# First phase of a decoder block on one core: x in four tiles of 4 KB rows, modulation rows between them, and half of x's transposes behind the first product

## The chip, the cores and the metric

The kernel runs on one core of a Trainium2 chip. The metric is the device time of one execution in microseconds (us). The engines are TensorE (PE in the profile, PEld for its weight loads), VectorE (DVE), ScalarE (ACT), GpSimd (POOL) and SyncE (SP), which issues most of the DMAs.

## What is computed

One layer of a residual decoder block for 512 tokens of width 1024 in float32. The change touches only the first lines: the norm, the modulation of x by the vector c, and the order in which the first projections start.

```
c_act = jax.nn.silu(c)
mod = c_act @ ada_w[l] + ada_b[l]
shift1, scale1, gate1, shift2, scale2, gate2 = ...
h = rms_norm(x, norm1_g[l]) * (1 + scale1) + shift1
z = h @ w_in[l]
q, k, v, p, g_attn, g_pool = jnp.split(z, split_at, axis=-1)
...
x = x + gate1 * (merged @ w_out[l])
...
x = x + gate2 * ((jax.nn.silu(u_g) * u_v) @ w_down[l])
```

## The kernel before, in words

All of it is one function, `block_kernel`. The instructions of PE, DVE and ACT stand on each engine in the order in which the code is written; an instruction that waits holds up all that stand behind it on its engine. SP's DMAs too are issued in the order of the code.

The first phase makes h, transposed: eight channel tiles k = 0 to 7 of 128 channels by 512 tokens. It runs so:

- x is loaded as four token tiles t = 0 to 3 of 128 rows, each in two halves of 512 channels (eight DMAs of 256 KB, line 154). `rms_rows` sums the squares of one half on ACT (L164) and of the other on DVE (L166), adds them (`ms`, L170) and raises to the power -1/2 on POOL (`rs`, L172). `scale_x` multiplies the halves by it (L210 and L214 on ACT, L212 on DVE).
- PE transposes 32 blocks of 128 by 128 (L232) into eight PSUM banks, xT_0 to xT_7. There are eight banks in all.
- The modulation is not a product on PE. silu(c), `crow`, is spread over the partitions by two small matmuls (`cb`, L220) and copied to `cbc`. Each of 16 rows of weights, `raw_ada`, of 513 KB, is multiplied by `cbc` and summed on DVE (`ada_sum`, L181). Its result is a column `acol`: g = 0 is the shift, g = 1 the scale, of channel tile k. Row (0, k) is loaded as `raw_ada_k` and row (1, k) as `raw_ada_(8+k)`.
- `make_x(k)` copies xT_k out of PSUM with the norm's gain (`xs_k`, L238 on ACT, and L240 on DVE for k = 7). `make_h(k)` applies scale and shift (L270) and rounds to the high part `h_k_h` (L272), both on ACT; `lo_h(k)` subtracts on DVE for the low part `h_k_l` (L277). For k = 0 gain and scale are one factor, `gs`.
- The projections p and q need weights in the same two parts: `hi_of` rounds a raw tile (`hi_p0`, L97 or L99), and a subtraction gives `lo_p0` (L109). A product is three matmuls: high by high (L125 for p and q), high by low, low by high (L128).
- PE then runs, for k = 0 to 7, twelve matmuls of p (four banks p_0 to p_3) and twelve of q (banks q_0 to q_3), and goes on with the projection k (L118 to L120).

The raw tiles (`raw_ada`, `raw_p`, `raw_q`, `crow`) share five buffers. `pump` issues the next load of a written list, `queue`, as soon as one of them is given free by `ada_sum` or `split`. The subtraction of q1's weights is on POOL (`pool=("q1",)`); four memsets of `kz` come later on the same engine.

Of the kernel before, what the change touches and what calls it, by code (L numbers as in the profile page):

```python
# [48 lines left out]
def block_kernel(tc, x, cvec, ada, wtok, wch, pool_w, wbr, wout, wup, wdn, pack, table, out):  # L49
# [4 lines left out]
    with ctx:  # L54
# [91 lines left out]
        acol = cpool.tile([P, 48], F32, name="acol")  # L146


        xt = []
        for t in range(TT):  # L150
            row = []
            for f in range(2):
                xi = slot(f"x_{t}_{f}")
                nc.sync.dma_start(xi, x[t * P : (t + 1) * P, f * 512 : (f + 1) * 512])
                row.append(xi)
            xt.append(row)

        def rms_rows(tiles, name):

            ss = mini.tile([P, 2], F32, tag="ss", name=f"ss_{name}")  # L160
            for f in range(2):
                junk = slot(f"junk_{name}_{f}")
                if f == 0:
                    nc.scalar.activation(junk, tiles[f], AF.Square, scale=1.0 / math.sqrt(D), accum_out=ss[:, f : f + 1])  # L164
                else:
                    nc.vector.tensor_tensor_reduce(  # L166
                        out=junk, in0=tiles[f], in1=tiles[f], op0=ALU.mult, op1=ALU.add, scale=1.0 / D,
                        scalar=EPS, accum_out=ss[:, f : f + 1])
            ms = mini.tile([P, 1], F32, tag="ms", name=f"ms_{name}")
# [37 lines left out]
        rss, cbs = [], []

        def scale_x(t):
            nc.scalar.activation(xt[t][0], xt[t][0], AF.Copy, scale=rss[t])  # L210
            if t < TT - 1:
                nc.vector.tensor_scalar(xt[t][1], xt[t][1], rss[t], None, op0=ALU.mult)  # L212
            else:
                nc.scalar.activation(xt[t][1], xt[t][1], AF.Copy, scale=rss[t])  # L214

        for t in range(TT):
            rs = rms_rows(xt[t], f"x{t}")
            if t < 2:
                cbs.append(bank(f"cb_{t}"))
                nc.tensor.matmul(cbs[t], ones, crow[:, t * 512 : t * 512 + 512], start=True, stop=True)  # L220
            if t:
                scale_x(t - 1)
                if t < 3:
                    nc.scalar.activation(cbc[:, (t - 1) * 512 : t * 512], cbs[t - 1], AF.Copy)
            rss.append(rs)
        scale_x(TT - 1)

        hh, hl, xs, araw = [], [], {}, {}
        xT = [bank(f"xT_{k}") for k in range(KT)]
        for t in range(TT):  # L230
            for k in range(KT):
                nc.tensor.transpose(  # L232
                    xT[k][:, tslice(t)], xt[t][k // 4][:, (k % 4) * P : (k % 4 + 1) * P], ident)

        def make_x(k):
            xs[k] = slot(f"xs_{k}")
            if k < KT - 1:
                nc.scalar.activation(xs[k], xT[k], AF.Copy, scale=col(C_N1 + k))  # L238
            else:
                nc.vector.tensor_scalar(xs[k], xT[k], col(C_N1 + k), None, op0=ALU.mult)  # L240


        queue = [(0, 0), (1, 0), "p0", "q0", (0, 1), (1, 1), (0, 2), (1, 2), "p1", "q1", (0, 3), (1, 3),
                 (0, 4), (1, 4), (0, 5), (1, 5), "p2", "q2", (0, 6), (1, 6), (0, 7), (1, 7), "p3", "q3"]
        held = [0]

        def pump():
            while queue and held[0] < 5:
                it = queue.pop(0)
                if isinstance(it, str):  # L250
                    early[it] = load_unit(plan[pos[it]][0], it)
                else:
                    araw[it] = ada_load(it[0], it[1])
                held[0] += 1

        def sum_h(k):
            for g in range(2):
                ada_sum(g, k, araw[g, k])
                held[0] -= 1
                pump()  # L260

        def split(name, **kw):
            ahead(name, 0, pool=("q1",), **kw)
            held[0] -= 1
            pump()

        def make_h(k, src=None, scale=None):
            hi = slot(f"h_{k}_h", F32R)
            lo = slot(f"h_{k}_l", F32R)
            nc.scalar.activation(xs[k], xs[k] if src is None else src, AF.Identity,  # L270
                                 scale=acols(1, k) if scale is None else scale, bias=acols(0, k))
            nc.scalar.activation(hi, xs[k], AF.Copy)  # L272
            hh.append(hi)
            hl.append(lo)

        def lo_h(k):
# [608 lines left out]
```

## Time and profile before

| | us |
|---|---|
| median of 3 runs (lowest to highest) | 691.81 (691.68 to 691.94) |
| the profiled execution, its own time | 691.4 |
| its span, first to last instruction | 689.6 |
| PE busy in the span | 677.6 (98%) |
| DVE busy | 443.2 (64%) |
| ACT busy | 304.4 (44%) |
| POOL busy | 59.4 (9%) |
| bytes moved by DMA | 94.50 MB, 137 GB/s over the span |

PE is the engine that is nearly always busy. The other shares are means over stages that differ, so they don't tell who is waited for at the start.

### The profile page before, as it was taken

To read this page: it belongs to the slowest core of one execution; us is meant where nothing else is said; L and a number is where in the kernel's file an instruction comes from. 1 tells how busy PE (TensorE), PEld (TensorE's weight loads), DVE (VectorE), ACT (ScalarE), POOL (GpSimd) and SP (SyncE) were. 2 spreads that over 40 slices of the span, in tenths; PEclk is the share of its full clock that TensorE was granted. 3 is DMA by queue.
4 is the path that set the end of the run, shared out by engine and by line. 5 is a ranking of instruction groups with operands and counts; after the bars stand their busy time and mean duration, and the time that the engine had idled before them with its cause. 6 is when DMAs were issued, how large, how long until landed. Compare 5 with 4: busy or idle time off the path is not lost.

```text
span 689.6 us, 8494 instructions
## 1 busy us (share of the span) xinstructions
PE 677.6 (98%) x3238; PEld 566.5 (82%) x3238; DVE 443.2 (64%) x719; ACT 304.4 (44%) x490; POOL 59.4 (9%) x60
## 2 busy tenths in 40 slices
PE   6999999999999999999999999999999999999997
PEld 4788788888888788889988888888888888888886
DVE  5786776887878788786575767676565653225213
ACT  6555347666555556315653434435343442211110
POOL 2203140000000155311000000000000000000000
PEclk9999999999999999999999999999999999999999
DMA  8795241454542466750313354442323324224001
GB/s 307 277 337 201 71 143 43 145 191 138 150 141 93 155 227 203 244 210 32 122 62 122 99 177 131 145 159 86 122 85 100 113 71 153 92 92 152 31 1 61
DMA packets 27631, 94.50 MB, mean 137 GB/s; under 512 B 3283, under 2 KB 3708, under 8 KB 27590
## 3 DMA queue, kind: packets, MB, share of 16 engines
q1 hardware_dynamic: 26198, 89.63, 38.1%
q0 software_dynamic: 1392, 4.33, 2.2%
q8 instruction: 25, 0.41, 0.2%
q14 instruction: 16, 0.13, 0.1%
HBM read 91.83 MB, written 2.12 MB: 136 GB/s over the span
## 4 chain that ended last, share of the span: by engine, by line
PE 94%; DMA 2%; ACT 1%; DVE 1%; SPq 1%; issue 1%; DVEq 0%; ACTq 0%
PE u L119 12%; PE u L120 12%; PE u L118 12%; PE d L118 6%; PE d L119 6%; PE d L120 6%; PE gate_ps L120 4%; PE gate_ps L119 4%; PE gate_ps L118 4%; PE o L118 2%; PE o L119 2%; PE o L120 2%; DMA raw_ada<-in_ada 2%; PE O L485 2%; PE p L128 1%; PE q L128 1%
## 5 line engine op out<-in xcount | busy, mean ns | idle before, releaser
L118 PE MATMUL u<-h2h,hi_up 128*128 128x512 f32 (+1 forms) x384 | 142.7, 372 | 0.0
L119 PE MATMUL u<-h2l,hi_up 128*128 128x512 f32 (+1 forms) x384 | 142.6, 371 | 0.0
L120 PE MATMUL u<-h2h,lo_up 128*128 128x512 f32 (+1 forms) x384 | 142.6, 371 | 0.0
L118 PEld LDWEIGHTS u<-h2h,hi_up 128*128 128x128 f32 x384 | 72.3, 188 | 12.6
L119 PEld LDWEIGHTS u<-h2l,hi_up 128*128 128x128 f32 x384 | 72.3, 188 | 12.5
L120 PEld LDWEIGHTS u<-h2h,lo_up 128*128 128x128 f32 x384 | 72.3, 188 | 12.3
L118 PE MATMUL d<-hi_dn,y_h 128*128 128x512 f32 (+1 forms) x198 | 72.6, 367 | 0.0
L119 PE MATMUL d<-lo_dn,y_h 128*128 128x512 f32 (+1 forms) x198 | 72.6, 367 | 0.0
L120 PE MATMUL d<-hi_dn,y_l 128*128 128x512 f32 (+1 forms) x198 | 72.4, 365 | 0.0
L109 DVE TENSOR_TENSOR lo_dn<-raw_dn,hi_dn 128x1024 fp32r<-128x1024 f32 x22 | 26.6, 1224 | 61.6 <-ACT hi_dn L99 61.6
L181 DVE CUSTOM_DVE_ANT_0 raw_ada<-raw_ada,cbc 128x1026 f32<-128x1026 f32 x48 | 61.1, 1292 | 3.3 <-DMA raw_ada<-in_ada 3.3
L109 DVE TENSOR_TENSOR lo_up<-raw_up,hi_up 128x1024 fp32r<-128x1024 f32 x44 | 52.1, 1221 | 8.7 <-ACT hi_up L99 8.7
L99 ACT ACTIVATE hi_dn<-raw_dn 128x1024 fp32r<-128x1024 f32 x22 | 23.0, 1059 | 75.0 <-PE d L120 66.2
L740 ACT ACTIVATE uv<-u,pk 128x512 f32<-128x512 f32 x22 | 17.2, 780 | 87.5 <-PE u L120 87.5
L741 DVE SCALAR_TENSOR_TENSOR uv<-u,pk,uv 128x511 f32<-128x511 f32 x22 | 16.5, 749 | 52.9 <-ACT uv L740 52.9
L120 PE MATMUL gate_ps<-h_h,lo_gate 128*128 128x512 f32 x128 | 49.9, 390 | 0.0
L119 PE MATMUL gate_ps<-h_l,hi_gate 128*128 128x512 f32 x128 | 49.9, 390 | 0.0
L118 PE MATMUL gate_ps<-h_h,hi_gate 128*128 128x512 f32 x128 | 49.9, 390 | 0.0
L99 ACT ACTIVATE hi_up<-raw_up 128x1024 fp32r<-128x1024 f32 x44 | 44.1, 1047 | 4.3 <-PE u L119 4.3
L118 PEld LDWEIGHTS d<-hi_dn,y_h 128*128 128x128 f32 x198 | 37.4, 189 | 6.2
L120 PEld LDWEIGHTS d<-hi_dn,y_l 128*128 128x128 f32 x198 | 37.3, 188 | 6.2
L119 PEld LDWEIGHTS d<-lo_dn,y_h 128*128 128x128 f32 x198 | 37.4, 189 | 6.1
(202 smaller groups left out, 1234.3 us busy)
## 6 DMA issues: line engine op xcount, KB each, us to landing
raw_ada<-in_ada SPq DMA_DIRECT2D x48, 513.0 KB, 4.8
raw_up<-in_wup SPq DMA_DIRECT2D x44, 512.0 KB, 4.3
raw_dn<-in_wdn SPq DMA_DIRECT2D x22, 512.0 KB, 3.3
raw_gate<-in_wch SPq DMA_DIRECT2D x16, 512.0 KB, 5.0
raw_br<-in_wbr SPq DMA_DIRECT2D x8, 512.0 KB, 4.4
raw_wo<-in_wout SPq DMA_DIRECT2D x8, 512.0 KB, 3.2
x<-in_x SPq DMA_DIRECT2D x8, 256.0 KB, 4.2
raw_p<-in_wtok SPq DMA_DIRECT2D x4, 512.0 KB, 5.9
```

The source lines that it names most:

```text
L99: nc.scalar.activation(hi, raw, AF.Copy)
L109: (nc.gpsimd if nm in pool else nc.vector).tensor_sub(lo, raw, hi.bitcast(F32))
L118: nc.tensor.matmul(ps, sh, mh, start=start, stop=False)
L119: nc.tensor.matmul(ps, sh, ml, start=False, stop=False)
L120: nc.tensor.matmul(ps, sl, mh, start=False, stop=stop)
L128: nc.tensor.matmul(ps, sl if i else sh, mh if i else ml, start=False, stop=stop and i != late)
L181: nc.vector.tensor_tensor_reduce(out=raw, in0=raw, in1=cbc, op0=ALU.mult, op1=ALU.add, scale=1.0, scalar=0.0, accum_out=acol[:, i : i + 1])
L485: nc.tensor.matmul(ops[:, kt * P :], lw, m[b_][:, o : o + w], start=(i == 0 and j == 0), stop=(i == 3 and j == 1))
L740: nc.scalar.activation(t, ps, AF.Identity, scale=cw(2), bias=col(C_CB + i))
L741: nc.vector.scalar_tensor_tensor(t[:, 1:], ps[:, : S - 1], cw(1), t[:, 1:], op0=ALU.mult, op1=ALU.add)
```

## The change

x comes as four DMAs of 512 KB with rows of 4 KB, into buffers of the pools for high and low weight parts, which are still free then. The order of loads becomes x_0, x_1, the modulation rows (0, 0) and (1, 0), x_2, x_3, p0, q0. The code of the phase is written anew in another order: the first modulation sums stand between the norm's sums of x; only the blocks of channel tiles 0 to 3 are transposed ahead of p's k = 0, and those of 4 to 7 stand behind it (`flip_x(t, 4)`), in the banks that held xT_0 to xT_3. `make_x(4)` to `make_x(7)` stand behind those. p's k = 0 takes its low weights ahead of the low part of h (`late`). The rounding of q0 goes from ACT to DVE, the subtraction of q1 from POOL to DVE. For k = 0 high part and value both come straight from PSUM, one on ACT (L300) and one on DVE (L304).

```diff
-            for f in range(2):
-                xi = slot(f"x_{t}_{f}")
-                nc.sync.dma_start(xi, x[t * P : (t + 1) * P, f * 512 : (f + 1) * 512])
...
+            xi = (whi_p if t < 2 else wlo_p).tile([P, 1024], F32, tag="hi" if t < 2 else "lo", name=f"x_{t}")
+            nc.sync.dma_start(xi, x[t * P : (t + 1) * P])
...
-        queue = [(0, 0), (1, 0), "p0", "q0", (0, 1), (1, 1), (0, 2), (1, 2), "p1", "q1", (0, 3), (1, 3),
+        queue = [(0, 0), (1, 0), "x2", "x3", "p0", "q0", (0, 1), (1, 1), (0, 2), (1, 2), "p1", "q1", (0, 3), (1, 3),
...
-            ahead(name, 0, pool=("q1",), **kw)
+            ahead(name, 0, **kw)
...
+        def flip_x(t, k0):
+            for k in range(k0, k0 + 4):
+                nc.tensor.transpose(xT[k][:, tslice(t)], xt[t][:, k * P : (k + 1) * P], ident)
...
+        flip_x(0, 0)
+        flip_x(1, 0)
+        sum_one(0, 0)
+        rss.append(rms_rows(xh[2], "x2"))
+        sum_one(1, 0)
...
+        rss.append(rms_rows(xh[3], "x3"))
+        scale_x(2, 0, False)
+        his["p0"] = hi_of("p0", early["p0"], True)
+        scale_x(3, 0, True)
+        flip_x(2, 0)
+        flip_x(3, 0)
...
+        nc.scalar.activation(hh[0], xT[0], AF.Identity, scale=gs, bias=acols(0, 0))
+        scale_x(2, 1, False)
+        scale_x(3, 1, False)
+        split("p0")
+        nc.vector.tensor_scalar(xs[0], xT[0], gs, acols(0, 0), op0=ALU.mult, op1=ALU.add)
         lo_h(0)
-        for k in range(1, KT):
-            if k == 5:
-                his["q0"] = hi_of("q0", early["q0"])
+        for k in range(1, 4):
             make_x(k)
         sum_h(1)
+        his["q0"] = hi_of("q0", early["q0"], True)
         split("q0")
         make_h(1)
         lo_h(1)
         sum_h(2)
-        qps = [bank(f"q_{t}") for t in range(TT)]
         pps = [bank(f"p_{g}") for g in range(TT)]
...
+            if k == 0:
+                for k2 in range(4, KT):
+                    xT[k2] = bank(f"xT_{k2}")
+                for t in range(TT):
+                    flip_x(t, 4)
+                for k2 in range(4, KT):
+                    make_x(k2, k2 == 7)
+                qps = [bank(f"q_{t}") for t in range(TT)]
```

What this makes of the order is shown at three places. In the rows the text after "<-" is what is read, the numbers behind the names are buffer numbers, and the brackets name the engines and DMA lanes that the instruction waits for. The first place is PE where p's k = 0 ends and q's begins. Before:

```order
L128 MATMUL p_2_272<-h_0_h_218,lo_p0_224 128x512
L128 MATMUL p_3_273<-h_0_h_218,lo_p0_224 128x512
L125 MATMUL q_0_266<-hi_q0_237,h_0_h_218 128x512 [waits Activation_49]
L125 MATMUL q_1_267<-hi_q0_237,h_0_h_218 128x512
L125 MATMUL q_2_268<-hi_q0_237,h_0_h_218 128x512 [waits Activation_49]
L125 MATMUL q_3_269<-hi_q0_237,h_0_h_218 128x512 [waits Activation_49]
L128 MATMUL q_0_266<-hi_q0_237,h_0_l_219 128x512
```

Now, with the last eight of the sixteen moved transposes:

```order
L259 MATMUL xT_4_246<-pk_80,x_2_101 128x128
L259 MATMUL xT_5_247<-pk_80,x_2_101 128x128
L259 MATMUL xT_6_248<-pk_80,x_2_101 128x128
L259 MATMUL xT_7_249<-pk_80,x_2_101 128x128
L259 MATMUL xT_4_246<-pk_80,x_3_103 128x128
L259 MATMUL xT_5_247<-pk_80,x_3_103 128x128
L259 MATMUL xT_6_248<-pk_80,x_3_103 128x128
L259 MATMUL xT_7_249<-pk_80,x_3_103 128x128
L125 MATMUL q_0_274<-hi_q0_213,h_0_h_190 128x512 [waits DVE_49,Activation_49]
L125 MATMUL q_1_275<-hi_q0_213,h_0_h_190 128x512 [waits Activation_49]
L125 MATMUL q_2_276<-hi_q0_213,h_0_h_190 128x512 [waits Activation_49]
L125 MATMUL q_3_277<-hi_q0_213,h_0_h_190 128x512 [waits DVE_49]
```

The transposes of channel tiles 4 to 7 now stand between p's k = 0 and q's k = 0, and q's banks are those of xT_4 to xT_7: the first matmul into q_3 waits for DVE, which copies xT_7 out.

The second place is DVE from the low part of h's tile 0 to the first sum of k = 2. Before:

```order
L277 TENSOR_TENSOR h_0_l_219<-xs_0_217,h_0_h_218 128x512 [waits Activation_49]
L240 TENSOR_SCALAR xs_7_243<-xT_7_166,pk_80 128x512 [waits PE_49]
L181 ISA raw_ada_1_207,acol_91<-raw_ada_1_207,cbc_81 128x1026 [waits DMAHW5_49]
L181 ISA acol_91 128x1
L181 ISA raw_ada_9_210,acol_91<-raw_ada_9_210,cbc_81 128x1026 [waits DMAHW7_49]
L181 ISA acol_91 128x1
L109 TENSOR_TENSOR lo_q0_251<-raw_q0_205,hi_q0_237 128x1024 [waits DMAHW4_49,Activation_49]
L277 TENSOR_TENSOR h_1_l_256<-xs_1_229,h_1_h_255 128x512 [waits Activation_49]
L181 ISA raw_ada_2_213,acol_91<-raw_ada_2_213,cbc_81 128x1026 [waits DMAHW0_49]
```

Now:

```order
L255 TENSOR_TENSOR h_0_l_191<-xs_0_189,h_0_h_190 128x512 [waits DVE_49]
L181 ISA raw_ada_1_109,acol_91<-raw_ada_1_109,cbc_81 128x1026 [waits DMAHW2_49]
L181 ISA acol_91 128x1
L181 ISA raw_ada_9_152,acol_91<-raw_ada_9_152,cbc_81 128x1026 [waits DMAHW3_49]
L181 ISA acol_91 128x1
L97 CAST hi_q0_213<-raw_q0_107 128x1024 [waits DMAHW0_49]
L109 TENSOR_TENSOR lo_q0_215<-raw_q0_107,hi_q0_213 128x1024 [waits DVE_49]
L255 TENSOR_TENSOR h_1_l_220<-xs_1_201,h_1_h_219 128x512 [waits Activation_49]
L181 ISA raw_ada_2_164,acol_91<-raw_ada_2_164,cbc_81 128x1026 [waits DMAHW4_49]
L181 ISA acol_91 128x1
L181 ISA raw_ada_10_197,acol_91<-raw_ada_10_197,cbc_81 128x1026 [waits DMAHW5_49]
L242 TENSOR_SCALAR xs_7_272<-xT_7_249,pk_80 128x512 [waits PE_49]
```

The copy of xT_7 (`xs_7`) stood ahead of the sums of k = 1; it now stands behind the sums of k = 1 and of k = 2, behind q0's rounding and both q0's and h_1's subtractions.

The third place is SP's list of loads from the third half tile of x on. Before:

```order
L154 DMA x_1_0_96<-in_x 128x512
L154 DMA x_1_1_98<-in_x 128x512
L154 DMA x_2_0_100<-in_x 128x512
L154 DMA x_2_1_102<-in_x 128x512
L154 DMA x_3_0_104<-in_x 128x512
L154 DMA x_3_1_106<-in_x 128x512 [waits DMAHW0_49]
L74 DMA raw_ada_0_199<-in_ada 128x1026 [waits DMAHW1_49]
L74 DMA raw_ada_8_201<-in_ada 128x1026 [waits DMAHW2_49]
L74 DMA raw_p0_203<-in_wtok 128x1024 [waits DMAHW3_49]
```

Now, from the second tile of x on:

```order
L153 DMA x_1_95<-in_x 128x1024
L74 DMA raw_ada_0_97<-in_ada 128x1026
L74 DMA raw_ada_8_99<-in_ada 128x1026
L153 DMA x_2_101<-in_x 128x1024
L153 DMA x_3_103<-in_x 128x1024
L74 DMA raw_p0_105<-in_wtok 128x1024
L74 DMA raw_q0_107<-in_wtok 128x1024 [waits DMAHW0_49]
```

The two modulation rows of k = 0 now stand ahead of the second half of x; the bytes ahead of p0 are the same as before.

## Rows read from the trace of the kernel before

**Rows 1.** The page: busy time, share of the span and instructions of each engine.
```profile
PE 677.6 (98%) x3238; PEld 566.5 (82%) x3238; DVE 443.2 (64%) x719; ACT 304.4 (44%) x490; POOL 59.4 (9%) x60
```

**Rows 2.** Stretches: us, busy us of each engine (instructions), PE clock, DMA share, GB/s.
```profile
22.65:62.14 39.49, 38.58 (x170) 31.31 (x168) 28.33 (x38) 19.07 (x25) 4.46 (x5) 1.00 0.83 297
62.14:685.00 622.86, 622.61 (x3011) 524.05 (x3009) 399.23 (x646) 268.89 (x438) 51.30 (x46) 1.00 0.36 121
```

**Rows 3.** Timeline of PE: start, us, line, operation, count [idle before <-releaser].
```profile
16.06 2.10 PE L125 MATMUL p<-h_h,hi_p 128*128 128x512 f32 x4 [1.56 <-ACT h_h L272]
22.65 1.07 PE L125 MATMUL p<-h_h,hi_p 128*128 128x512 f32 x4
...
28.09 1.07 PE L125 MATMUL p<-h_h,hi_p 128*128 128x512 f32 x4
...
34.60 1.20 PE L125 MATMUL p<-h_h,hi_p 128*128 128x512 f32 x4 [0.91 <-ACT h_h L272]
...
62.14 0.39 PE L118 MATMUL k<-hi_k,h_h 128*128 128x512 f32 x1
```

**Rows 4.** Timeline of DVE, norm of x and first sums.
```profile
7.01 0.69 DVE L166 CUSTOM_DVE_ANT_0 junk_x<-x 128x512 f32<-128x512 f32 x1 [0.44 <-DMA x<-in_x]
...
8.39 0.69 DVE L166 CUSTOM_DVE_ANT_0 junk_x<-x 128x512 f32<-128x512 f32 x1
...
9.27 0.48 DVE L212 TENSOR_SCALAR x<-x,rs_x 128x512 f32<-128x512 f32 x1
...
11.59 1.23 DVE L181 CUSTOM_DVE_ANT_0 raw_ada<-raw_ada,cbc 128x1026 f32<-128x1026 f32 x1 [0.23 <-DMA raw_ada<-in_ada]
...
13.04 1.23 DVE L181 CUSTOM_DVE_ANT_0 raw_ada<-raw_ada,cbc 128x1026 f32<-128x1026 f32 x1 [0.22 <-DMA raw_ada<-in_ada]
```

**Rows 5.** Timeline of DVE, on from there.
```profile
14.39 0.69 DVE L97 CAST hi_p<-raw_p 128x1024 fp32r<-128x1024 f32 x1
15.11 1.23 DVE L109 TENSOR_TENSOR lo_p<-raw_p,hi_p 128x1024 fp32r<-128x1024 f32 x1
16.25 0.68 DVE L277 TENSOR_TENSOR h_l<-xs,h_h 128x512 fp32r<-128x512 f32 x1
16.86 0.74 DVE L240 TENSOR_SCALAR xs<-xT,pk 128x512 f32<-128x512 f32 x1
17.52 1.22 DVE L181 CUSTOM_DVE_ANT_0 raw_ada<-raw_ada,cbc 128x1026 f32<-128x1026 f32 x1
...
19.81 1.22 DVE L109 TENSOR_TENSOR lo_q<-raw_q,hi_q 128x1024 fp32r<-128x1024 f32 x1
21.83 0.69 DVE L277 TENSOR_TENSOR h_l<-xs,h_h 128x512 fp32r<-128x512 f32 x1 [0.80 <-ACT h_h L272]
22.43 1.22 DVE L181 CUSTOM_DVE_ANT_0 raw_ada<-raw_ada,cbc 128x1026 f32<-128x1026 f32 x1
```

**Rows 6.** Timeline of ACT: second half of cbc, h of k = 0, copies out of PSUM.
```profile
9.57 0.58 ACT L224 ACTIVATE cbc<-cb 128x512 f32<-128x512 f32 x1
...
14.57 0.78 ACT L270 ACTIVATE xs<-xT,acol,gs 128x512 f32<-128x512 f32 x1 [1.44 <-PE xT L232]
...
15.92 2.41 ACT L238 ACTIVATE xs<-xT,pk 128x512 f32<-128x512 f32 x4
```

**Rows 7.** Stretches of the tile xT alone, columns as in rows 2 without POOL.
```profile
10.20:12.80 2.60, 2.59 (x12) 2.59 (x13) 0.00 (x0) 0.00 (x0) 1.00 0.83 333
13.00:14.40 1.40, 1.40 (x14) 1.26 (x12) 0.00 (x0) 0.00 (x0) 1.00 1.03 421
```

**Rows 8.** Timeline of POOL and DVE around 28 us.
```profile
28.31 2.49 POOL L109 TENSOR_TENSOR lo_q<-raw_q,hi_q 128x1024 fp32r<-128x1024 f32 x1 [16.55 <-ACT hi_q L99]
28.46 3.43 DVE L181 CUSTOM_DVE_ANT_0 raw_ada<-raw_ada,cbc 128x1026 f32<-128x1026 f32 x1
30.86 2.03 POOL L390 MEMSET kz<- 64x512 f32 x4
31.81 1.22 DVE L181 CUSTOM_DVE_ANT_0 raw_ada<-raw_ada,cbc 128x1026 f32<-128x1026 f32 x1
```

More of the change, by code (lines that the diff above doesn't have):

```diff
@@ L146, in block_kernel, with load_x @@
         acol = cpool.tile([P, 48], F32, name="acol")
-        xt = []
-        for t in range(TT):
-            row = []
-            for f in range(2):
-                xi = slot(f"x_{t}_{f}")
-                nc.sync.dma_start(xi, x[t * P : (t + 1) * P, f * 512 : (f + 1) * 512])
-                row.append(xi)
-            xt.append(row)
+        xt, xh = [], []
+        def load_x(t):
+            xi = (whi_p if t < 2 else wlo_p).tile([P, 1024], F32, tag="hi" if t < 2 else "lo", name=f"x_{t}")
+            nc.sync.dma_start(xi, x[t * P : (t + 1) * P])
+            xt.append(xi)
+            xh.append([xi[:, :512], xi[:, 512:]])
         def rms_rows(tiles, name):
+            ms = mini.tile([P, 1], F32, tag="ms", name=f"ms_{name}")
             ss = mini.tile([P, 2], F32, tag="ss", name=f"ss_{name}")
@@ L163, in rms_rows @@
                 if f == 0:
-                    nc.scalar.activation(junk, tiles[f], AF.Square, scale=1.0 / math.sqrt(D), accum_out=ss[:, f : f + 1])
+                    nc.scalar.activation(
+                        junk, tiles[f], AF.Square, scale=1.0 / math.sqrt(D), accum_out=ss[:, f : f + 1])
                 else:
@@ L168, in rms_rows @@
                         scalar=EPS, accum_out=ss[:, f : f + 1])
-            ms = mini.tile([P, 1], F32, tag="ms", name=f"ms_{name}")
             nc.vector.tensor_add(ms, ss[:, 0:1], ss[:, 1:2])
@@ L205, in bias_table @@
                 nc.gpsimd.dma_start(fd[:, c0 : c0 + n], fsb[i][:H, :n])
[L207 to L226, printed above, removed]
-        hh, hl, xs, araw = [], [], {}, {}
[L229 to L240, printed above, removed]
-        queue = [(0, 0), (1, 0), "p0", "q0", (0, 1), (1, 1), (0, 2), (1, 2), "p1", "q1", (0, 3), (1, 3),
+        hh, hl, xs, araw = [], [], {}, {}
+        queue = [(0, 0), (1, 0), "x2", "x3", "p0", "q0", (0, 1), (1, 1), (0, 2), (1, 2), "p1", "q1", (0, 3), (1, 3),
                  (0, 4), (1, 4), (0, 5), (1, 5), "p2", "q2", (0, 6), (1, 6), (0, 7), (1, 7), "p3", "q3"]
@@ L249, in pump @@
                 it = queue.pop(0)
+                if it in ("x2", "x3"):
+                    load_x(int(it[1]))
+                    continue
                 if isinstance(it, str):
@@ L254, in pump, with sum_one, make_x, make_h @@
                 held[0] += 1
+        def sum_one(g, k):
+            ada_sum(g, k, araw[g, k])
+            held[0] -= 1
+            pump()
         def sum_h(k):
             for g in range(2):
-                ada_sum(g, k, araw[g, k])
-                held[0] -= 1
-                pump()
+                sum_one(g, k)
         def split(name, **kw):
-            ahead(name, 0, pool=("q1",), **kw)
+            ahead(name, 0, **kw)
             held[0] -= 1
             pump()
-        def make_h(k, src=None, scale=None):
+        def make_x(k, on_dve=False):
+            xs[k] = slot(f"xs_{k}")
+            if on_dve:
+                nc.vector.tensor_scalar(xs[k], xT[k], col(C_N1 + k), None, op0=ALU.mult)
+            else:
+                nc.scalar.activation(xs[k], xT[k], AF.Copy, scale=col(C_N1 + k))
+        def make_h(k):
             hi = slot(f"h_{k}_h", F32R)
             lo = slot(f"h_{k}_l", F32R)
-            nc.scalar.activation(xs[k], xs[k] if src is None else src, AF.Identity,
-                                 scale=acols(1, k) if scale is None else scale, bias=acols(0, k))
+            nc.scalar.activation(xs[k], xs[k], AF.Identity, scale=acols(1, k), bias=acols(0, k))
             nc.scalar.activation(hi, xs[k], AF.Copy)
@@ L277, in lo_h, with scale_x @@
             nc.vector.tensor_sub(hl[k], xs[k], hh[k].bitcast(F32))
-        pump()
-        sum_h(0)
+        def flip_x(t, k0):
+            for k in range(k0, k0 + 4):
+                nc.tensor.transpose(xT[k][:, tslice(t)], xt[t][:, k * P : (k + 1) * P], ident)
+        def scale_x(t, f, on_dve):
+            if on_dve:
+                nc.vector.tensor_scalar(xh[t][f], xh[t][f], rss[t], None, op0=ALU.mult)
+            else:
+                nc.scalar.activation(xh[t][f], xh[t][f], AF.Copy, scale=rss[t])
+        load_x(0)
+        load_x(1)
+        pump()
+        rss, xT = [], {}
+        rss.append(rms_rows(xh[0], "x0"))
+        cbs = [bank("cb_0"), bank("cb_1")]
+        for f in range(2):
+            nc.tensor.matmul(cbs[f], ones, crow[:, f * 512 : f * 512 + 512], start=True, stop=True)
+        rss.append(rms_rows(xh[1], "x1"))
+        nc.scalar.activation(cbc[:, :512], cbs[0], AF.Copy)
+        scale_x(0, 0, False)
+        scale_x(0, 1, True)
+        nc.scalar.activation(cbc[:, 512:1024], cbs[1], AF.Copy)
+        scale_x(1, 0, False)
+        scale_x(1, 1, True)
+        for k in range(4):
+            xT[k] = bank(f"xT_{k}")
+        flip_x(0, 0)
[3 more added lines that the diff above has]
+        sum_one(1, 0)
         gs = mini.tile([P, 1], F32, tag="gs", name="gs")
         nc.vector.tensor_mul(gs, acols(1, 0), col(C_N1))
-        xs[0] = slot("xs_0")
-        make_h(0, xT[0], gs)
-        split("p0", on_dve=True)
+        rss.append(rms_rows(xh[3], "x3"))
[4 more added lines that the diff above has]
+        flip_x(3, 0)
+        xs[0] = slot("xs_0")
+        hh.append(slot("h_0_h", F32R))
+        hl.append(slot("h_0_l", F32R))
+        nc.scalar.activation(hh[0], xT[0], AF.Identity, scale=gs, bias=acols(0, 0))
[3 more added lines that the diff above has]
+        nc.vector.tensor_scalar(xs[0], xT[0], gs, acols(0, 0), op0=ALU.mult, op1=ALU.add)
         lo_h(0)
-        for k in range(1, KT):
-            if k == 5:
-                his["q0"] = hi_of("q0", early["q0"])
+        for k in range(1, 4):
             make_x(k)
         sum_h(1)
+        his["q0"] = hi_of("q0", early["q0"], True)
         split("q0")
@@ L304, in block_kernel @@
             cs = [slice(c0 + g * P, c0 + (g + 1) * P) for g in range(TT)]
-            mm3s([(pps[g], pw[0][:, cs[g]], pw[1][:, cs[g]], hh[k], hl[k]) for g in range(TT)], k == 0, k == KT - 1)
+            mm3s([(pps[g], pw[0][:, cs[g]], pw[1][:, cs[g]], hh[k], hl[k]) for g in range(TT)], k == 0, k == KT - 1,
+                 late=k == 0)
+            if k == 0:
[6 more added lines that the diff above has]
+                qps = [bank(f"q_{t}") for t in range(TT)]
             if k + 2 < KT:
```

## The prediction, made blind

> **What bounds the kernel now.** I read the page first, then the time by stretches, then the timelines of PE, DVE and ACT up to 62 us. The page has PE busy for 98% [rows 1], so the question is only where PE is not. By stretches it is busy 622.61 of 622.86 us from the first matmul of the projection k, at 62.14, to 685 [rows 2]: from there on the kernel is PE's own work, which the change leaves alone. Behind 685 comes only the output. So the time moves one for one with the start of that matmul, and only what happens ahead of 62.14 is looked at.
>
> There PE starts p's k = 0 at 16.06 and p's k = 1 at 22.65 [rows 3]. From 22.65 to 28.09 stand 24 matmuls, 0.227 us each. From p's k = 1 to the end of q's k = 7 there are 14 groups of 12, 168 matmuls, 38.1 us; the stretch takes 39.49 [rows 2]. The missing 1.4 us are stalls, of which the row at 34.60 shows 0.91, behind `h_h` on ACT [rows 3]. That wait has a cause that can be read: the sum ahead of it on DVE took 3.43 us where one takes 1.22, next to the subtraction of q1 on POOL [rows 5, 8].
>
> The work to be moved is DVE's. It has few gaps from 11.59 on: sums of `raw_ada`, roundings, subtractions [rows 4, 5]. The reader is to see in rows 5 that the copy of xT_7 stands at 16.86, ahead of four sums, and that PE needs nothing from DVE for the first matmuls of q.
>
> **The loads.** Eight DMAs of 256 KB become four of 512 KB; bytes stay. Before, the first 1 MB had landed at 7.01, where DVE's wait for x1 ends [rows 4]; x_0 and x_1 are the same bytes, so 7.0 again. The two halves of DVE's wait for modulation rows show the pace: 13.04 - 11.59 = 1.45 us for 513 KB [rows 4]. Now x_0, x_1, (0, 0), (1, 0) and x_2 make 2.56 MB, as many as x and (0, 0) made before, which had landed at 11.59. By bytes x_2 lands at 11.55; as a lower bound, three transfers behind 7.0 at 1.28 us each (412 GB/s, the pace of 421 GB/s in rows 7 with a little loss) end at 10.8. I take 11.3, x_3 at 12.7, p0 at about 14.1. Fewer DMAs save SP issue time that nobody waits for, since the loads behind are queued anyway. Rows of 4 KB I cost at nothing.
>
> **DVE's chain in the new order.** The first sum needs `cbc`, whose second half was copied from 9.57 to 10.15, with one more Square ahead of it on ACT than now [rows 6]; with 1.15 us for a sum (half of 19.81 - 17.52 for two, [rows 5]) it is over by 11.3 even so. From there each step is the distance to the next row:
> - x_2's squares and their addition, 8.39 to 9.27: 0.88, until 12.2 [rows 4].
> - Sum (1, 0) and `gs`, 13.04 to 14.39: 1.35, until 13.55 [rows 4, 5].
> - x_3's squares: 0.88, until 14.45. Rounding p0, 14.39 to 15.11: 0.72, until 15.15. Scaling half of x_3: 0.48, until 15.65 [rows 4, 5].
> - `lo_p0`, 15.11 to 16.25: 1.14, until 16.8. PE meanwhile transposes x_3's four blocks, and ACT makes `h_0_h` in 0.78, until about 16.8 too [rows 6]. So p's k = 0 starts at about 16.8, later than the 16.06 of before.
> - `xs_0` and `h_0_l`: 0.66 + 0.61, until 18.1 (the steps 16.86 to 17.52 and 16.25 to 16.86, [rows 5]).
> - Sums (0, 1), (1, 1): 2.29, until 20.4. Rounding q0, new on DVE: 0.72, until 21.1. `lo_q0`: 1.14, until 22.25. `h_1_l`, 21.83 to 22.43: 0.6, until 22.85 [rows 5].
> - Sums (0, 2), (1, 2): 2.3, until 25.15. Only then the copy of xT_7: 0.74, until 25.9 [rows 5].
>
> **PE behind it.** The banks of q are those of xT_4 to xT_7, so q_3's first matmul waits for 25.9. PE without that wait: p's k = 0 from 16.8 with 12 x 0.227 = 2.7 until 19.5, 16 transposes at 0.1 us (14 in 1.40, [rows 7]) until 21.2, three copies on ACT at 0.6 (2.41 for four, [rows 6]) until about 22.9. So DVE is the last by 3 us, and whatever is earlier ahead of it is lost. After 25.9 come q_3 and eight more matmuls of q, 9 x 0.227 = 2.05: p's k = 1 starts at 28.0, against 22.65. That is 5.35 us lost. Of it the later stalls give back 1.4: `h_3` needs sums (0, 3), (1, 3), two subtractions and `h_2_l` on DVE behind 25.9, about 8 us, until 34, and PE asks for it at 28.0 + 2 x 5.44 = 38.9. With so much room nothing later waits, and POOL's subtraction is gone. The projection k starts at 28.0 + 38.1 = 66.1, which is 3.95 later than 62.14.
>
> The profiled execution took 691.4, so it would take 695.35; the median of before lies 0.4 higher, so about **695.7 us** on the median's scale. An unknown that I cost at nothing: the four memsets of `kz` on POOL (2.03 us) now run at about 15 to 17, beside DVE's scaling of x_3 and `lo_p0`. The nearest rows are a sum beside the last memset, 1.22 as ever, and the sum beside a subtraction on POOL, 3.43 [rows 8]; a memset is nearer to the first, so 0, with 2.2 as the upper end.
>
> **The clock, an edit's cover.** The PE clock column reads 1.00 everywhere, but transposes of one shape take 2.59/12 = 0.216 us up to 12.8 and 1.40/14 = 0.1 from 13.0 [rows 7]: the lower level (1.2 GHz) and the upper (2.4). It rose while PE had transposed without a pause since 10.2. Now PE has only four transposes at a time ahead of p's k = 0, with pauses between, so p's k = 0 may begin at the lower level: 12 x 0.454 = 5.45 until 22.25. With transposes at the upper level (until 24) and copies it stays under 25.9, hidden by the wait for DVE. The Trainium skill, "TensorE: Matmul & The Clock Gate", section "Part 4: PE-mode transpose", has it that transposes do not count as activity for the clock gate as matmuls do. This trace disagrees, since the clock rose amid nothing but transposes; by the rule the sum would be that of the first rival.
>
> **Rivals.**
> - The clock stays low through the transposes too: 22.25 + 16 x 0.216 = 25.7, the last copies on ACT until 26.9, q_3 at 27.2, and p's k = 1 at 29.2 (eight matmuls at the upper level) to 31.0 (all at the lower). That adds 1.2 to 3 us: about 697.3. For it speaks that the transposes before p are sparse now; against it that rows 7 show the rise inside 2.8 us of unbroken transposes.
> - Faster. The first sum no longer waits for all of x, and could start up to 2 us sooner than 11.59. If DVE kept such a lead and more, the wait for xT_7 would be gone. The point that decides is 62.14 - 38.1 - 2.05 = 22.0: the copy must be over by then, 3.9 us sooner than I find. DVE's own work from 11.3 to 25.9 has no idle time to give, so only earlier landings could, and those are bound at 10.8. With everything 2 us early and no stalls it would be 691.8 - 2 - 1.4 = 688.4.
> - No change: the stall removed (1.4 us) and a shorter wait cancel. It needs the copy over at 20.6 to 23.4, for about 692; x_2 at its earliest gives 25.4.
>
> **Chances and range.** The wait for DVE as summed 0.70 (694.2 to 696.6: landings of x 0.5 us to either side, 0.6 for semaphores and steps, memsets up); low clock or memsets beside it 0.18 (696.6 to 699); no change 0.07; faster 0.04; something worse 0.01. Range with 8 in 10: 694.2 to 698.0. A measurement of this kernel can tell 0.2%, 1.4 us, from no change: faster 0.04, same 0.07, slower 0.89.
>
> **What would show it.** Right: on PE a wait of 2 us or more in front of an L125 matmul into q, ended by DVE `xs` at L242; that copy at about 25; p's k = 1 at 28; no waits of PE from there to 66; DVE's sums at about 1.22 all through. Wrong: `xs_7` over before 23, or PE waiting again between 30 and 60, or p's k = 0 at well over 17 us, which would mean that x_2 and x_3 land later than their bytes say.

## The result, and the profile after

The changed kernel takes 697.1 us (median of 4 runs, 696.49 to 698.2) against 691.74 (691.43 to 691.94): a ratio of 1.008 with a 95% interval of 1.0062 to 1.0097, so slower by 5.4 us. The profiled execution took 696.58, with a span of 694.8; against that of before that is 5.2 more.

In the profiled executions all of it lies ahead of the projection k, which starts 5.31 us later. The page's busy row and two stretches of the changed kernel (columns as in rows 2) show it:

```profile
PE 679.5 (98%) x3238; PEld 567.3 (82%) x3238; DVE 444.0 (64%) x722; ACT 303.0 (44%) x488; POOL 58.1 (8%) x59
```

```profile
29.37:67.45 38.08, 38.08 (x170) 31.54 (x168) 24.14 (x34) 16.33 (x22) 0.00 (x0) 1.00 0.73 274
67.45:690.50 623.05, 622.79 (x3011) 523.99 (x3009) 399.20 (x646) 268.72 (x438) 51.26 (x46) 1.00 0.36 121
```

The second stretch has the same 3011 matmuls as that of [rows 2] and takes 623.05 against 622.86. The first is p's k = 1 to the projection k: 38.08 against 39.49, with no idle time on PE, so the stall of 0.91 is gone as forecast. The loss is made before p's k = 1, which starts at 29.37 against 22.65 [rows 3]. Three timelines and the loads show how. PE first:

```profile
14.78 1.11 PE L259 MATMUL xT<-pk,x 128*128 128x128 f32 x4 [4.75 <-ACT x L265]
16.57 1.11 PE L259 MATMUL xT<-pk,x 128*128 128x128 f32 x4 [0.67 <-DVE x L263]
17.91 2.07 PE L125 MATMUL p<-h_h,hi_p 128*128 128x512 f32 x4 [0.23 <-ACT h_h L300]
19.78 1.91 PE L128 MATMUL p<-h_h,lo_p 128*128 128x512 f32 x4
21.49 1.34 PE L128 MATMUL p<-h_l,hi_p 128*128 128x512 f32 x4
22.66 1.91 PE L259 MATMUL xT<-pk,x 128*128 128x128 f32 x16
25.02 1.66 PE L125 MATMUL q<-hi_q,h_h 128*128 128x512 f32 x3 [0.45 <-ACT xs L244]
27.20 0.50 PE L125 MATMUL q<-hi_q,h_h 128*128 128x512 f32 x1 [0.52 <-DVE xs L242]
...
29.37 1.07 PE L125 MATMUL p<-h_h,hi_p 128*128 128x512 f32 x4
...
67.45 0.39 PE L118 MATMUL k<-hi_k,h_h 128*128 128x512 f32 x1
```

q_3's matmul at 27.20 waits for DVE's copy at L242, as forecast. But PE had little time to wait: p's k = 0 began at 17.91 and its second four matmuls took 21.49 - 19.78 = 1.71 us, nearly twice 4 x 0.227. That is the lower level of the clock, although the column of the granted clock reads 1.00 there, as this stretch of the changed kernel shows (nine matmuls in 3.80 us):

```profile
18.00:21.80 3.80, 3.80 (x9) 3.02 (x10) 3.77 (x7) 2.81 (x5) 0.01 (x1) 1.00 0.65 201
```

DVE, with the steps that the forecast named:

```profile
5.95 0.69 DVE L167 CUSTOM_DVE_ANT_0 junk_x<-x 128x512 f32<-128x512 f32 x1 [0.58 <-DMA x<-in_x]
...
11.45 0.69 DVE L167 CUSTOM_DVE_ANT_0 junk_x<-x 128x512 f32<-128x512 f32 x1 [1.94 <-DMA x<-in_x]
...
14.56 0.69 DVE L97 CAST hi_p<-raw_p 128x1024 fp32r<-128x1024 f32 x1
15.68 0.83 DVE L263 TENSOR_SCALAR x<-x,rs_x 128x512 f32<-128x512 f32 x1 [0.44 <-POOL rs_x L172]
...
17.89 0.81 DVE L304 TENSOR_SCALAR xs<-xT,gs,acol 128x512 f32<-128x512 f32 x1 [0.25 <-ACT h_h L300]
...
19.34 1.22 DVE L181 CUSTOM_DVE_ANT_0 raw_ada<-raw_ada,cbc 128x1026 f32<-128x1026 f32 x1
...
26.40 0.74 DVE L242 TENSOR_SCALAR xs<-xT,pk 128x512 f32<-128x512 f32 x1
```

The wait of 1.94 us at 11.45 is the one for x_2, which landed as forecast (11.3); the others are small. What counts is that the sum at 19.34 was forecast for 18.1. POOL in the same time:

```profile
12.50 1.47 POOL L172 TENSOR_TENSOR rs_x<-ms_x,mhalf 128x1 f32<-128x1 f32 x1 [4.78 <-DVE ms_x L170]
14.72 0.93 POOL L172 TENSOR_TENSOR rs_x<-ms_x,mhalf 128x1 f32<-128x1 f32 x1 [0.75 <-DVE ms_x L170]
15.71 2.30 POOL L415 MEMSET kz<- 64x512 f32 x4
```

And the loads, as stretches of the changed kernel (the last column is GB/s, the one before it the DMA share):

```profile
2.00:5.00 3.00, 1.74 (x2) 0.83 (x3) 0.60 (x1) 1.67 (x4) 0.00 (x0) 1.00 0.95 352
5.00:9.00 4.00, 3.23 (x8) 1.14 (x7) 2.73 (x9) 3.03 (x8) 1.29 (x2) 1.00 0.65 256
9.00:12.00 3.00, 1.02 (x4) 0.62 (x4) 1.06 (x3) 0.55 (x2) 0.00 (x0) 1.00 1.00 406
```

x_1 was there at 5.95, 1.06 us sooner than the same bytes in [rows 4] (7.01), and that lead was lost again while the two modulation rows came, at 256 GB/s with the DMA engines a third idle.

### The profile page after: what moved, and what is told of

Its sections match the earlier page's. It is cut to its first block, busy times and chain, and to the rows that moved or that the text cites. A ratio compares the mean times of both kernels' runs of the same rounds, so it can differ in the third digit from the quotient of the medians.

```text
span 694.8 us, 8488 instructions
## 1 busy us (share of the span) xinstructions
PE 679.5 (98%) x3238; PEld 567.3 (82%) x3238; DVE 444.0 (64%) x722; ACT 303.0 (44%) x488; POOL 58.1 (8%) x59
## 4 chain that ended last, share of the span: by engine, by line
PE 95%; DVE 2%; DMA 1%; SPq 0%; issue 0%; ACT 0%; POOL 0%; DVEq 0%
PE u L119 12%; PE u L118 12%; PE u L120 12%; PE d L118 6%; PE d L119 6%; PE d L120 6%; PE gate_ps L119 4%; PE gate_ps L118 4%; PE gate_ps L120 4%; PE o L118 2%; PE o L120 2%; PE q L128 2%; PE o L119 2%; PE p L128 2%; PE O L510 2%; DMA x<-in_x 1%
## 5 line engine op out<-in xcount | busy, mean ns | idle before, releaser
L181 DVE CUSTOM_DVE_ANT_0 raw_ada<-raw_ada,cbc 128x1026 f32<-128x1026 f32 x48 | 58.9, 1247 | 3.0 <-DMA raw_ada<-in_ada 2.9
L766 DVE SCALAR_TENSOR_TENSOR uv<-u,pk,uv 128x511 f32<-128x511 f32 x22 | 16.5, 749 | 52.9 <-ACT uv L765 52.9
```

The lines of the kernel that those rows point to most:

```text
L181: nc.vector.tensor_tensor_reduce(out=raw, in0=raw, in1=cbc, op0=ALU.mult, op1=ALU.add, scale=1.0, scalar=0.0, accum_out=acol[:, i : i + 1])
L766: nc.vector.scalar_tensor_tensor(t[:, 1:], ps[:, : S - 1], cw(1), t[:, 1:], op0=ALU.mult, op1=ALU.add)
```

## The experiments

All times are medians; each kernel was timed against the kernel before on the same chip, and the ratio is given as its 95% interval. The kernel before itself had medians of 691.37 to 691.74 in these, so a difference of under 0.4 us between two rows of the table says nothing by itself. The two starts are from the profiled execution.

| kernel | us | ratio to before | p's k = 0 | projection k |
|---|---|---|---|---|
| before | 691.74 | 1 | 16.06 | 62.14 |
| after | 697.1 | 1.0062 to 1.0097 | 17.91 | 67.45 |
| after, copy of xT_7 ahead of k = 2's sums | 695.33 | 1.0044 to 1.0069 | 17.91 | 66.19 |
| after, idle transposes that raise the clock | 698.99 | 1.009 to 1.0121 | 17.72 | 69.95 |
| after, both of these | 694.34 | 1.003 to 1.0055 | 17.77 | 65.25 |
| after, kz memsets early | 696.9 | 1.0066 to 1.0093 | 18.10 | 69.00 |
| after, all transposes ahead of p | 693.2 | 1.0015 to 1.0036 | 18.59 | 63.87 |
| before, q1's subtraction on DVE | 690.73 | 0.9984 to 1.0001 | 15.83 | 61.90 |
| before, x in 4 KB rows | 690.82 | 0.9985 to 1.0002 | 15.56 | 61.67 |
| before, both of these ("the fastest kernel") | 689.89 | 0.9969 to 0.9986 | 15.57 | 60.76 |
| the fastest kernel, modulation rows ahead of x_2 | 693.84 | 1.002 to 1.0042 | 18.42 | 63.91 |
| the fastest kernel, h_0 from PSUM | 691.65 | 0.999 to 1.0008 | 16.53 | 62.07 |

### Is the wait for the copy of xT_7 what ends last?

```diff
         lo_h(1)
-        sum_h(2)
...
                     make_x(k2, k2 == 7)
+                sum_h(2)
```

> The changed kernel with the copy of xT_7 on DVE ahead of the sums (0, 2) and (1, 2). Theory A (two waits one behind the other: the copy on DVE, and just ahead of it p's k = 0 at the lower clock with the transposes and three copies on ACT behind it): q_3 starts at about 26.4 instead of 27.2, 0.8 us are gained, about 696.3. Theory B (only the place of the copy on DVE counts, PE would be ready 3 us sooner): 2.5 to 3 us are gained, about 694.3.

Measured: 695.33, 1.8 less than the changed kernel. On PE the wait for L242 is gone, and the matmuls of q go through:

```profile
24.79 1.66 PE L125 MATMUL q<-hi_q,h_h 128*128 128x512 f32 x4 [0.45 <-ACT xs L244]
...
28.11 1.07 PE L125 MATMUL p<-h_h,hi_p 128*128 128x512 f32 x4
```

So the copy did end last, but only by 29.37 - 28.11 = 1.26 us, of which 0.23 is that PE's transposes behind p's k = 0 began sooner in this execution (22.43 for 22.66). Close behind the copy stood PE itself, held up by its clock, and ACT's copies.

### Is the low clock that second bound?

```diff
         flip_x(1, 0)
+        for _ in range(20):
+            nc.tensor.transpose(cbs[0][:, :P], ident, ident)
...
         flip_x(2, 0)
+        for _ in range(4):
+            nc.tensor.transpose(cbs[0][:, :P], ident, ident)
```

> The changed kernel with 24 more transposes of the identity into a bank that is read no more, in PE's pauses before and between those of x_2 and x_3, so that the clock may rise before p's k = 0; they add no result. Theory A: the clock is up at p's k = 0, its twelve matmuls take 2.7 instead of 4.8 us, but q_3 still waits for the copy on DVE; 0.2 to 0.5 us are gained, about 696.8. Theory C (the lower clock alone made the loss over the forecast): 1.5 to 2 us are gained, about 695.3.

Measured: 698.99, slower than without, which none of the theories had. PE's timeline of this kernel, and then two of its stretches:

```profile
17.72 1.20 PE L125 MATMUL p<-h_h,hi_p 128*128 128x512 f32 x4 [0.54 <-ACT h_h L304]
...
23.73 1.65 PE L125 MATMUL q<-hi_q,h_h 128*128 128x512 f32 x3 [1.24 <-ACT xs L244]
27.01 0.80 PE L125 MATMUL q<-hi_q,h_h 128*128 128x512 f32 x1 [1.63 <-DVE xs L242]
27.61 1.91 PE L128 MATMUL q<-hi_q,h_l 128*128 128x512 f32 x4
```

```profile
13.00:25.90 12.90, 8.53 (x48) 6.08 (x46) 12.14 (x21) 8.02 (x14) 4.11 (x6) 1.00 0.87 319
26.00:32.60 6.60, 5.59 (x13) 4.44 (x14) 5.46 (x9) 3.34 (x4) 0.00 (x0) 0.50 0.74 260
```

The transposes did their part: p's k = 0 ran at the upper level. But PE came sooner to the same waits: 1.24 us for ACT's copies and then, three matmuls later, 1.63 us for DVE's. From then on the granted clock is 0.50, for thirteen matmuls. A faster engine in front of a wait that it doesn't end gains nothing, and here the longer waits were followed by a lower clock. That they are its cause no run shows by itself; two kernels further down bear on it, one with a single wait of 1.23 us and no fall, one with 0.45 and 1.49 us and a fall.

### Both together

The two edits above in one kernel.

> Both edits together. Theory A: each hides the other, so together they gain more than the sum of the two: q's k = 0 runs behind the third copy on ACT at about 25.2, about 2 us gained, 695.1. If either alone were the cause, both together give what that one gives.

Measured: 694.34, 2.8 less than the changed kernel, and its runs lie within 0.08 us. PE waits for ACT's copies alone:

```profile
23.78 1.72 PE L125 MATMUL q<-hi_q,h_h 128*128 128x512 f32 x4 [1.23 <-ACT xs L244]
```

p's k = 1 starts at 27.17 instead of 29.37. So 2.2 us of the loss are the copy and the clock together. Some 3 us over the kernel before remain (694.34 against 691.37).

### Do the memsets of kz disturb DVE?

```diff
+        kz = {}
+        for e in range(2):
+            for i in range(2):
+                z = slot(f"kz_{e}_{i}", F32R)
+                nc.gpsimd.memset(z[64 - e * 64 : 128 - e * 64].bitcast(F32), 0.0)
+                kz[e, i] = z
         xt, xh = [], []
```

The same lines go out further down.

> The changed kernel with the four memsets of kz as the first work of POOL, long before the norm. Theory E (POOL and DVE hold each other up): DVE's scaling of x_3 takes 0.48 instead of 0.83, and since all behind it on DVE moves, the copy of xT_7 is over 0.3 to 0.4 us sooner; the time falls by as much, which is near what can be told. Rival: the 0.83 comes from something else and stays.

Measured: 696.9, which can't be told from 697.1: the four runs of this kernel lie between 696.09 and 698.06. The trace does answer the question, DVE first and POOL behind it:

```profile
16.22 0.48 DVE L269 TENSOR_SCALAR x<-x,rs_x 128x512 f32<-128x512 f32 x1 [0.44 <-POOL rs_x L178]
```

```profile
2.00 2.02 POOL L153 MEMSET kz<- 64x512 f32 x4
...
13.03 1.47 POOL L178 TENSOR_TENSOR rs_x<-ms_x,mhalf 128x1 f32<-128x1 f32 x1 [5.18 <-DVE ms_x L176]
15.25 0.93 POOL L178 TENSOR_TENSOR rs_x<-ms_x,mhalf 128x1 f32<-128x1 f32 x1 [0.75 <-DVE ms_x L176]
```

Scaling x_3 takes 0.48 again instead of 0.83, so the 0.35 was the memsets' doing; the two powers on POOL stay at 1.47 and 0.93, so those are not. In this profiled execution (698.06 us) x_2 landed at 11.99, 0.54 later than in that of the changed kernel, so what its copy of xT_7 gained can't be read off. Its 69.00 has another cause: PE reached q at 24.25, waited 1.49 us for the copy, and the stretch from 25.8 to 29.6 has a granted clock of 0.65, as in the kernel with idle transposes.

### Does the split of the transposes cost, or the order ahead of it?

All 32 transposes and the copies 1 to 7 go ahead of p's k = 0 again; loads and sums keep the changed order. The scalings of x_2's and x_3's other halves, which these transposes read, go ahead with them; that part of the edit is not shown.

```diff
-        for k in range(4):
+        for k in range(KT):
             xT[k] = bank(f"xT_{k}")
-        flip_x(0, 0)
-        flip_x(1, 0)
+        for t in range(2):
+            flip_x(t, 0)
+            flip_x(t, 4)
...
-        for k in range(1, 4):
-            make_x(k)
+        for k in range(1, KT):
+            make_x(k, k == 7)
```

> The changed kernel, its loads and sums, but with all 32 transposes ahead of p's k = 0, the copies 1 to 7 behind h_0 as before, and q's and p's banks as before. Theory A (the split of the transposes, with what waits behind it, makes most of the loss): p's k = 1 starts at 25 to 26 instead of 29.4, 3.5 to 4.5 us are gained, about 693. Theory D (the new order of loads and sums makes it): under 1.5 us gained, 695.6 or more.

Measured: 693.2, 3.9 less than the changed kernel. p's k = 0 starts 0.68 later than there, at 18.59, and yet the projection k comes at 63.87, 3.58 sooner: behind p's k = 0 PE waits only once more, 0.4 us. So 3.58 of the 5.31 us, two thirds, go with the split. What is left, 1.73 us at the projection k, is lost in spite of q1's subtraction being on DVE, so the order ahead of it has a price too.

### The parts that could gain, on the kernel before

One word goes out for q1, four lines change for the rows of x, and the third kernel has both.

```diff
-            ahead(name, 0, pool=("q1",), **kw)
+            ahead(name, 0, **kw)
```

> The kernel before with one part of the change alone: the subtraction of q1 on DVE instead of POOL. Theory A: the sum beside it takes 1.22 instead of 3.43 us, PE's wait at 34.6 is gone, 1.0 to 1.4 us gained, about 690.5. Rival: DVE, which has one subtraction of 1.14 more, is late for another reason, and nothing is gained: 691.7.

```diff
-            row = []
-            for f in range(2):
-                xi = slot(f"x_{t}_{f}")
-                nc.sync.dma_start(xi, x[t * P : (t + 1) * P, f * 512 : (f + 1) * 512])
-                row.append(xi)
-            xt.append(row)
+            xi = (whi_p if t < 2 else wlo_p).tile([P, 1024], F32, tag="hi" if t < 2 else "lo", name=f"x_{t}")
+            nc.sync.dma_start(xi, x[t * P : (t + 1) * P])
+            xt.append([xi[:, :512], xi[:, 512:]])
```

> The kernel before with one part alone: x in four tiles of 4 KB rows, all of x first as before. The changed kernel had its first MB of x 1.07 us sooner, but p0's weights only 0.4 us sooner. Theory A: the lead is lost in the slow loads of the first modulation rows, 0.2 to 0.5 us gained, about 691.0. Rival: the lead is kept, 1 us gained, 690.4.

> The kernel before with two parts of the change: x in four tiles of 4 KB rows and the subtraction of q1 on DVE. If the gains add (0.6 from the second), about 690.3; if both only move up to the same next wait, 690.7.

Measured: 690.73, 690.82 and 689.89. Each part alone is 0.6 to 0.7 us and within what its interval tells from nothing; both together are 1.6 us and faster than the kernel before beyond doubt (0.9969 to 0.9986). q1 alone gives up its gain again: the stall at 34.60 [rows 3] is gone, and a wait stands further down on PE:

```profile
40.01 1.20 PE L125 MATMUL p<-h_h,hi_p 128*128 128x512 f32 x4 [0.97 <-ACT hi_p L99]
```

With the rows of 4 KB beside it, PE waits for nothing between p's k = 0 and the projection k.

### The order of loads by itself

On that fastest kernel, only the loads are put in the changed order; all work stands as in the kernel before.

```diff
+        araw = {(g, 0): ada_load(g, 0) for g in range(2)}
+        load_x(2)
+        load_x(3)
...
-        queue = [(0, 0), (1, 0), "p0", "q0", (0, 1), (1, 1), (0, 2), (1, 2), "p1", "q1", (0, 3), (1, 3),
+        queue = ["p0", "q0", (0, 1), (1, 1), (0, 2), (1, 2), "p1", "q1", (0, 3), (1, 3),
```

> The kernel before with x in four 4 KB tiles and q1's subtraction on DVE (689.89 us, p's k = 0 at 15.57, the projection k at 60.76), now with the changed kernel's order of loads alone: the modulation rows (0, 0) and (1, 0) between x_1 and x_2. All work keeps the order in which the kernel before has it, so DVE does both sums behind the squares of all of x. Theory A (the order of loads is what costs, in the changed kernel too: all of x is needed before p, and it now lands last): x_3 lands at about 12.7, its squares end at 13.6, the two sums at 15.9, h_0_h at 17.5, so p's k = 0 starts at 17.5, 2 us later, and the time is 691.9. Theory B (the order of loads is free, and what the changed kernel loses in this part is lost by its order of work): p's k = 0 at most 0.5 us later, at most 690.4.

Measured: 693.84, 3.95 more than 689.89. The loads' order costs, and more than the 2 us expected: p's k = 0 starts 2.85 later, and the projection k 3.15. One place shows on PE:

```profile
13.20 4.30 PE L237 MATMUL xT<-pk,x 128*128 128x128 f32 x25 [4.03 <-ACT cbc L229]
```

PE stands still for 4 us behind the first seven transposes: the eighth needs a bank that `cb` holds. In this order of work the copy of `cbc` that is named here is queued on ACT behind the squares of x_2, which had landed at 11.32 (DVE's wait for it ends there), and behind the scaling of x_1. DVE is as late as PE: its scalings, squares and sums end with `gs` at 16.83, and ACT starts h_0 at 16.92.

What h_0 needs is the same in both orders of loads, all of x and both modulation rows, and the last of it lands at nearly the same time. The order decides how much work is still to do then. In the fastest kernel the row (1, 0) lands last, and ACT starts h_0 1.52 us behind it:

```profile
12.55 1.23 DVE L178 CUSTOM_DVE_ANT_0 raw_ada<-raw_ada,cbc 128x1026 f32<-128x1026 f32 x1 [0.59 <-DMA raw_ada<-in_ada]
```

```profile
14.07 0.78 ACT L267 ACTIVATE xs<-xT,acol,gs 128x512 f32<-128x512 f32 x1 [1.49 <-DVE gs L280]
```

In the changed kernel x_3 lands last, and its squares, its power, its scaling and its transposes are still to come, with a sum and a rounding between them on DVE; ACT starts h_0 4.38 us behind it:

```profile
12.70 0.63 ACT L164 ACTIVATE junk_x<-x 128x512 f32<-128x512 f32 x1 [0.53 <-DMA x<-in_x]
...
17.08 0.78 ACT L300 ACTIVATE h_h<-xT,acol,gs 128x512 fp32r<-128x512 f32 x1 [2.35 <-PE xT L259]
```

That the changed kernel does its sums in the gap gains little back: with the same loads and its order of work, the kernel with all transposes ahead has the projection k at 63.87, against 63.91.

### Would h_0 straight from PSUM help?

```diff
-        make_h(0, xT[0], gs)
+        hh.append(slot("h_0_h", F32R))
+        hl.append(slot("h_0_l", F32R))
+        nc.scalar.activation(hh[0], xT[0], AF.Identity, scale=gs, bias=acols(0, 0))
         split("p0", on_dve=True)
+        nc.vector.tensor_scalar(xs[0], xT[0], gs, acols(0, 0), op0=ALU.mult, op1=ALU.add)
...
-            mm3s([(pps[g], pw[0][:, cs[g]], pw[1][:, cs[g]], hh[k], hl[k]) for g in range(TT)], k == 0, k == KT - 1)
+            mm3s([(pps[g], pw[0][:, cs[g]], pw[1][:, cs[g]], hh[k], hl[k]) for g in range(TT)], k == 0, k == KT - 1,
+                 late=k == 0)
```

> The kernel before with x in four 4 KB tiles, q1's subtraction on DVE (689.89 us), and now two more parts of the change that stand by themselves: the high part of h_0 comes straight from PSUM in one ACT operation, its value from a second read of PSUM on DVE, and p's k = 0 takes its low weights ahead of the low part of h. Theory A (ACT, which makes h_0_h and then frees p's banks by its copies, is what p's k = 0 waits for): h_0_h is ready one ACT operation sooner, about 0.65 us, and the copies behind it too, so p's k = 0 starts at 14.9 and the time is 689.2. Theory B (DVE takes over: it has 0.7 us more in front of h_0_l, and behind it stand the copy of xT_7 and the sums of k = 1 and 2): nothing or a loss of up to 0.7, 689.9 to 690.6.

Measured: 691.65, so some 1.7 worse than the fastest kernel, which it was to improve, and the projection k starts 1.31 later; neither theory had that much. PE:

```profile
16.53 0.96 PE L125 MATMUL p<-h_h,hi_p 128*128 128x512 f32 x3 [2.81 <-DVE xs L286]
17.92 0.50 PE L125 MATMUL p<-h_h,hi_p 128*128 128x512 f32 x1 [0.42 <-DVE xs L237]
```

`h_0_h` was ready 0.7 us sooner, as hoped. But p's banks are those of xT here, and the first of them now has a second reader, DVE, whose read at L286 stood behind both of p0's operations and ended at 16.5. In the changed kernel p's banks are other ones, so it doesn't pay this.

## Why the prediction was right, and by how much it was off

The time, 697.1, lies in the range, on the side that was forecast, and the copy of xT_7 on DVE is what ended last, as the first experiment shows. But 697.1 is outside the 694.2 to 696.6 that the summed case was given with 0.70; it lies in the band of the second case, low clock or memsets beside DVE, which had 0.18. Both of these did occur. The clock, though, was not low through the transposes, as the first rival has it, and the memsets explain only a quarter of a microsecond. What made the time longer than the sum is mostly waits on DVE's chain that the forecast left out, told below. So that the time falls into this band is in part luck.

Of the signs that were to show the forecast right, two held: PE has no wait from p's k = 1 to the projection k, and DVE's sums take 1.22 to 1.23 us. The main one failed: the wait in front of q for DVE was to be 2 us or more and is 0.52. One sign of being wrong came, p's k = 0 at 17.91, but not for the reason given, since x_2 and x_3 landed as forecast. The sizes were off at the following steps.

- **The landings** held, by two errors that cancel: x_2 at 11.45 (forecast 11.3), x_3 at 12.70 (12.7). Rows of 4 KB, costed at nothing, and fewer DMAs, whose saving on SP nobody was to wait for, together brought x_1 1.06 us sooner; the two modulation rows, at 256 GB/s, took that back.
- **DVE's chain until `hi_p0`** held: 14.56 (forecast 14.45). **From there to the first sum of k = 1** it took 4.78 us instead of 3.65. The 1.13 are four terms, up to rounding: 0.40 of waiting for x_3's power on POOL, a step that the forecast left out; 0.25 because scaling x_3 was slower (0.83 instead of 0.48 of busy time), which the memsets caused that were costed at 0 with an upper end of 2.2; 0.31 of waiting for `h_0_h`, whose bank was ready later, as x_3's transposes came behind that scaling and ran at the lower clock; and 0.18 for `xs_0`, which takes 0.84 to the next row where 0.66 was taken from a copy with one operation. From the sum to the end of the copy it took 7.80 where 7.8 was forecast.
- **The copy of xT_7** was over at 27.14 (forecast 25.9), p's k = 1 at 29.37 (28.0), the projection k at 67.45 (66.1). The stretch from one to the other took 38.08 (38.1).
- **What stands close behind.** The forecast gave PE 3 us of waiting for DVE. It waited 0.45 for ACT and 0.52 for DVE, because p's k = 0 began 1.1 later than forecast (17.91 for 16.8) and its first eight matmuls ran at the lower level: the first rival's condition held for these, and not for the sixteen transposes at 22.66, which took 1.91 at the upper one. So the two cases that were set against each other ended 1.26 us apart: taking away the copy alone gains no more than that at p's k = 1, and taking away the low clock alone can gain nothing, since the copy still ends last. In the kernel with idle transposes nothing but transposes was added, and p's first four matmuls took 1.20 instead of 2.07. The Trainium skill, "TensorE: Matmul & The Clock Gate", section "Part 4: PE-mode transpose", has it that transposes don't count for the clock as matmuls do; this disagrees, as [rows 7] did.
- **The part of the loss that the prediction didn't name as such.** It let DVE's chain start from x_2's landing, rightly, and so has the price of x_2's new place in its sum, but it never asked what that price was. By the projection k in the profiles the change is made up so: x in four DMAs of 4 KB rows, 62.14 to 61.67, a gain of 0.47; q1 on DVE, to 60.76, a gain of 0.91; the order of loads, to 63.91, a loss of 3.15; the order of work with all transposes ahead, to 63.87, nothing on balance; the split of the transposes, to 67.45, a loss of 3.58. The sum is 5.31, the whole difference. The rounding of q0 on DVE, the low weights first (`late`) and the two reads of xT_0 were not tested by themselves in the changed kernel. Each of these is a difference between two single executions, and the steps depend on the order in which they are taken.

Open is why the first two modulation rows come so slowly, in the changed order and in the old one alike: in the fastest kernel, too, the stretch from 9 to 12 us in which they come moved only 246 GB/s at a DMA share of 0.62. No run here tells.

## What to carry to other kernels

When banks or buffers are reused earlier than before, the reader that frees them comes onto the path of whoever reuses them: look up where that reader stands in its engine's order, and move it ahead of what nobody waits for yet. When the first product needs several loads, put last the one with the least work between its landing and that product: a modulation row left 1.52 us of it here, a tile of x 4.38. An edit of many parts is worth taking apart: two of the parts here made the kernel 1.6 us faster than before (689.89), and two lost 6.7 at the projection k.

## What the runs showed of the hardware

- A pause of PE can cost more than its length. With the clock up, waits of 1.24 and 1.63 us, three matmuls apart, were followed by a granted clock of 0.50 for 6.6 us, and waits of 0.45 and 1.49 us by 0.65 for 3.8 us (kz early). A single wait of 1.23 us was not (both edits), and in the fastest kernel a single wait of 1.91 us after 25 unbroken transposes did not bring it down: p's k = 0 went on at 1.09 for four matmuls behind it.
- The clock column of the stretches reads 1.00 also where the matmuls' own pace shows the lower level (the changed kernel up to about 22 us); one has to look at the matmuls' distance.
- POOL and DVE slow each other, and not only in large operations: four memsets took 2.30 us beside DVE's scaling and subtraction against 2.02 with DVE idle, and the scaling 0.83 against 0.48. The power of 128 values on POOL took 1.47 us where it began beside a sum on DVE and 0.93 where it began beside a rounding, against 0.72 where it began beside a scaling of x (fastest kernel). For the power this is read from the times alone; no run takes DVE's work away from it.
- x in four DMAs with rows of 4 KB, instead of eight with rows of 2 KB, had its first megabyte 0.92 us sooner (6.09 in the fastest kernel, 7.01 before). The rows and the number of DMAs changed together: SP issued the eight in 4.13 us and the four in 1.78, and no run parts the two.
